# High and low activation halves in one 512-column product, in both FFNs and layer 1's output projection

## The chip, the core and the metric

The kernel runs on one core of a Trainium2 chip. The metric is the device time of one execution in microseconds. Five engines run their own instruction streams in order and meet through semaphores: TensorE (PE; its weight loads have a row of their own, PEld), VectorE (DVE), ScalarE (ACT), GpSimd (POOL) and SyncE (SP, which here issues nearly all transfers).

## The reference

Two decoder layers over 256 tokens of width 2048, in float32. Layer 0 mixes tokens with RWKV-7 and Gated DeltaNet, layer 1 with Mamba-2; each mixer has an input and an output projection, and each layer ends in a SwiGLU feed-forward block (FFN) of hidden width 5632. Every sub-layer is normalised, scaled and shifted by vectors made from `c` and a weight matrix ("ada"), and added back through a gate. What the change touches is the FFN of both layers and the last line of the Mamba-2 mixer:

```python
def swiglu(h, w1, w3, w2):
    return (jax.nn.silu(h @ w1) * (h @ w3)) @ w2
...
    return y.astype(h.dtype) @ w_out          # mamba2_mix: 4096 -> 2048
...
        x = x + gate * y
        shift, scale, gate = ada_modulation(c, ada_ffn_w[i], ada_ffn_b[i])
        h = rms_norm(x) * (1.0 + scale) + shift
        x = x + gate * swiglu(h, ffn_w1[i], ffn_w3[i], ffn_w2[i])
```

## The kernel before

Activations lie with features on the 128 partitions and the 256 tokens (T) along the free side, so a matrix of width 2048 is 16 tiles of 128x256. Every large product is made in float32r, whose operands are rounded; to keep float32 accuracy each operand is split into a high and a low part, and a 128x128 weight tile is used in three matmuls of 256 columns: high weights by high activations, high weights by low activations, low weights by high activations. In the program `whi` and `wlo` are the parts of the weights, `hhi`/`hlo`, `ghi`/`glo`, `yhi`/`ylo` those of the activations (normed input, FFN hidden layer, second half of the mixer's output).

Weights stream from memory. `pieces` lists them in order of use; `issue_raw` has SP load each into one of five `raw` buffers; `split_next` has ScalarE copy a piece of up to 8 weight tiles (128x1024) into `whi`; `low_parts` has VectorE write `raw - whi` into `wlo`. There are three buffers each of `whi` and `wlo` (`PARTS`), so ScalarE's copy of a piece waits until TensorE has left the piece three before it. `products` writes the matmuls of a piece: for unit i (one weight tile) the two with `whi`, and LAG = 4 units later the one with `wlo`.

An FFN runs in two halves of 22 hidden tiles. The *up* stage makes, for each hidden tile, the gate and the value product (16 units each) in the two halves of one 512-column bank; ScalarE applies Silu to the gate (`fs`), VectorE multiplies (`fg`), and `split` makes `ghi` and `glo`. The first 8 of the 88 up products of each FFN run apart, in `lin_slab`, which goes through all eight per input tile while the input is still being normed; the change leaves them alone. The *down* stage makes 16 output tiles of 22 units each in the first half of a bank; `out_tiles` adds each to the residual `x` through the gate. Layer 1's output projection has 16 output tiles in each of two halves of 16 units.

Beside this, VectorE makes the ada vectors: 320 half rows `adat` of 128x1024, multiplied and summed by one custom instruction each, spread over layer 0, its FFN, the Mamba-2 mixer, layer 1's output projection and the start of layer 1's FFN.

The order of the instructions on each engine is fixed when the program is written: a `Clock` class with costs per instruction form decides how far ahead pieces are split (`SOON`), when an ada half row is put into VectorE's stream (`fill_ada`, which lets it in when VectorE is early by that clock, or when it is due) and when the mixers' step chains take a step (`run`). The costs count columns: a 512-column float32r matmul costs 217.6 ns in it, two of 256 columns 217.6 together. What the change adds to VectorE and ScalarE therefore also moves the ada rows and the steps of layer 1's mixer; layer 0's mixer stands as it was.

Of the kernel before, what the change touches and what calls it, by code (L numbers as in the profile page):

```python
# [395 lines left out]
def trunk(ctx: ExitStack, tc: tile.TileContext, I, out):  # L396
# [117 lines left out]
    hhi = cp.tile([P, KT, T], F32R, name="hhi")  # L514
    hlo = cp.tile([P, KT, T], F32R, name="hlo")
    h2 = (hhi, hlo)
# [232 lines left out]
    def products(units, hi, lo, o, act):  # L749

        ahi, alo = act
        n = len(units)
        lag = min(LAG, n)
        w = lambda t, i: t[:, (o + i) * P:(o + i + 1) * P]
        for i in range(n + lag):
            if i < n:
                ps, kt, a, z = units[i]
                PE.matmul(ps, w(hi, i), ahi[:, kt, :], start=a, stop=False)
                PE.matmul(ps, w(hi, i), alo[:, kt, :], start=False, stop=False)
            if i >= lag:  # L760
                ps, kt, a, z = units[i - lag]
                PE.matmul(ps, w(lo, i - lag), ahi[:, kt, :], start=False, stop=z)
            if i % STEP == STEP - 1 or i == n + lag - 1:
                low_parts()
                issue_raw()
                run()
                if max(clock.at(ET.DVE), clock.at(ET.Activation)) < clock.at(ET.PE) + SOON:
                    prefetch()
                fill_ada()
# [86 lines left out]
    def out_tiles(l, m, ps, x, nxt=None):  # L856

        ms = range(m, m + len(ps))
        for o, m in zip(ps, ms):
            V.scalar_tensor_tensor(x[:, m, :], o, modc(l, 2, m), x[:, m, :], ALU.mult, ALU.add)  # L860
# [16 lines left out]
    def ffn(l, x, told, tnew):  # L877
# [4 lines left out]
        with tc.tile_pool(name=f"ffn{l}", bufs=1, reuse_waits="tile") as fp:  # L882
            ghi = fp.tile([P, NHH, T], F32R, name=f"ghi{l}")
            glo = fp.tile([P, NHH, T], F32R, name=f"glo{l}")
            for half in range(2):
                for jj in range(NHH):
                    if pss:
                        ps = pss.pop(0)
                    else:
                        ps = bank(True)  # L890
                        for q in range(2):
                            lin_tile(ps[:, q * T:(q + 1) * T], h2, range(KT))
                    s = fp.tile([P, T], F32, tag="fs", name=nm("fs"), bufs=2)
                    g = fp.tile([P, T], F32, tag="fg", name=nm("fg"), bufs=2)
                    S.activation(s, ps[:, 0:T], AF.Silu)
                    V.tensor_tensor(g, s, ps[:, T:2 * T], ALU.mult)
                    release(ps)
                    split(ghi[:, jj, :], glo[:, jj, :], g)
                for m in range(16):
                    ps = bank(True)  # L900
                    for q in range(2):
                        lin_tile(ps[:, 0:T], (ghi, glo), range(11 * q, 11 * q + 11), q == 0, q == 1)
                    out_tiles(l, m, [ps[:, 0:T]], x, (l + 1, t) if half == 1 else None)
                    release(ps)
# [775 lines left out]
    def layer1(x, told):  # L1680
# [4 lines left out]
        with tc.tile_pool(name="y1", bufs=1, reuse_waits="tile") as yp:  # L1685
            ymix = yp.tile([P, 32, T], F32, name="ymix1")
            with tc.tile_pool(name="mx1", bufs=1, reuse_waits="tile") as mx:
# [3 lines left out]
                for m in range(16):  # L1691
                    ps = bank(True)
                    lin_tile(ps[:, 0:T], h2, range(KT))
                    out_tiles(2, m, [ps[:, 0:T]], x)
                    release(ps)
                drain()
            t = open_x("t1")
            with tc.tile_pool(name="yo1", bufs=1, reuse_waits="tile") as fp:
                yhi = fp.tile([P, KT, T], F32R, name="yhi1")
                ylo = fp.tile([P, KT, T], F32R, name="ylo1")  # L1700
                for kt in range(KT):
                    split(yhi[:, kt, :], ylo[:, kt, :], ymix[:, 16 + kt, :])
                for m in range(16):
                    ps = bank(True)
                    lin_tile(ps[:, 0:T], (yhi, ylo), range(KT))
                    out_tiles(2, m, [ps[:, 0:T]], x, (3, t))
# [273 lines left out]
```

## Time and profile before

| | us |
|---|---|
| median of 3 runs (lowest, highest) | 3013.86 (3011.43, 3022.01) |
| the profiled execution: its own time | 3014.75 |
| its span | 3012.9 |
| mean granted TensorE clock | 0.981 of full speed |

| stage (us from the start) | PE busy | DVE busy | ACT busy |
|---|---|---|---|
| FFN 0, up, first half (840 to 1040) | 200.00 | 149.36 | 86.66 |
| FFN 0, down, first half (1040 to 1160) | 120.00 | 100.34 | 49.05 |
| FFN 0, up, second half (1160 to 1410) | 250.00 | 176.25 | 108.26 |
| Mamba-2 mixer (1560 to 2100) | 533.63 | 447.14 | 319.73 |
| layer 1's output projection (2120 to 2240) | 119.21 | 91.98 | 59.13 |
| FFN 1, up, second half (2630 to 2870) | 240.00 | 120.60 | 105.04 |
| FFN 1, down, second half (2870 to 2995) | 125.00 | 68.28 | 61.08 |

Since matmuls overlap in the records (one of 281 ns starts every 117 ns or so), "busy" only says that TensorE had no hole there; how fast it went is read from the number of matmuls in a stretch. Nearly all instructions are recorded under one line, L372 of the helper that keeps the order, so groups are told apart by the tiles that they write and read.

### The profile page before, as it was taken

Reading aid. Unit: us, or ns where it says so; the run is one execution under the profiler, and the core shown is the slowest. Engines: PE = TensorE matmul, PEld = TensorE weight load, DVE = VectorE, ACT = ScalarE, POOL = GpSimd, SP = SyncE. Lnnn points to the kernel's source line nnn. Section 1 sums busy time; section 2 is a strip of 40 time slices with the busy share of each in tenths; the row PEclk is TensorE's granted clock in tenths of the full one; section 3 lists DMA queues with packets and bytes.
Section 4 is the critical chain, followed back from the end, with each engine's and each line's share of the span. In section 5 each row is a group of like instructions: output and inputs, shape, how many; then the busy total and the mean of one; then the engine's idle time right before and its main releaser. Section 6 shows DMA issues by size and latency. Waiting matters only on the chain.

```text
span 3012.9 us, 61369 instructions
## 1 busy us (share of the span) xinstructions
PE 2884.7 (96%) x25095; PEld 2816.0 (93%) x25095; DVE 2199.6 (73%) x3438; ACT 1440.2 (48%) x2358; POOL 172.5 (6%) x191
## 2 busy tenths in 40 slices
PE   6789999998799999999999999999999999999998
PEld 6788889888699999999999999999999999999998
DVE  6987888888677787677768878888867745554555
ACT  3354546544344444444456556555445444444444
POOL 3400101100000000000000111111000000000000
PEclk9998999999899999999999999999999999999999
DMA  9865565577687898877865666666866755655554
GB/s 396 345 199 176 173 221 162 174 251 260 223 320 278 286 332 308 285 270 261 261 221 200 207 213 229 214 233 218 281 225 236 273 185 174 200 184 191 185 174 153
DMA packets 236730, 706.29 MB, mean 234 GB/s; under 512 B 36848, under 2 KB 55584, under 8 KB 236192
## 3 DMA queue, kind: packets, MB, share of 16 engines
q1 hardware_dynamic: 235872, 699.46, 67.9%
q8 instruction: 196, 3.21, 0.4%
q10 hardware_dynamic: 576, 2.92, 0.2%
q14 instruction: 86, 0.70, 0.1%
HBM read 695.70 MB, written 6.58 MB: 233 GB/s over the span
## 4 chain that ended last, share of the span: by engine, by line
issue 52%; PE 21%; DVE 2%; ACT 1%; DMA 0%; POOL 0%; DVEq 0%; POOLq 0%; ACTq 0%
PE bank L372 21%; DVE wlo L372 1%; ACT whi L372 0%; DMA adat<-in_ada 0%; DVE w L372 0%; DVE ymix L372 0%; DVE x L372 0%; POOL mgsa L372 0%; ACT mar L372 0%; DVE adat L372 0%; DVE mar L372 0%; ACT t L372 0%; DVE mxs L372 0%; DVE hlo L372 0%; DVE t0b L372 0%
## 5 line engine op out<-in xcount | busy, mean ns | idle before, releaser
L372 PE MATMUL bank<-hhi,whi 128*128 128x256 f32 x5568 | 1477.5, 287 | 35.3 <-ACT whi L372 33.9
L372 PE MATMUL bank<-hlo,whi 128*128 128x256 f32 x5568 | 1455.1, 283 | 6.9 <-DVE hlo L372 6.9
L372 DVE TENSOR_TENSOR wlo<-raw,whi 128x1024 fp32r<-128x1024 f32 (+3 forms) x1001 | 1112.5, 1125 | 438.8 <-ACT whi L372 433.6
L372 ACT ACTIVATE whi<-raw 128x1024 fp32r<-128x1024 f32 (+3 forms) x1001 | 967.9, 975 | 683.5 <-PE bank L372 659.5
L372 PE MATMUL bank<-hhi,wlo 128*128 128x256 f32 x5568 | 1126.6, 284 | 31.1 <-DVE wlo L372 30.9
L372 PEld LDWEIGHTS bank<-hhi,whi 128*128 128x128 f32 x5568 | 1064.0, 191 | 53.9 <-ACT whi L372 39.6
L372 PEld LDWEIGHTS bank<-hlo,whi 128*128 128x128 f32 x5568 | 1063.9, 191 | 10.4 <-DVE hlo L372 8.5
L372 PEld LDWEIGHTS bank<-hhi,wlo 128*128 128x128 f32 x5568 | 861.8, 190 | 41.7 <-DVE wlo L372 36.1
L372 PE MATMUL bank<-glo,whi 128*128 128x256 f32 x1408 | 351.1, 281 | 0.0
L372 PE MATMUL bank<-ghi,whi 128*128 128x256 f32 x1408 | 351.0, 281 | 0.0
L372 PEld LDWEIGHTS bank<-glo,whi 128*128 128x128 f32 x1408 | 265.0, 188 | 0.0
L372 PEld LDWEIGHTS bank<-ghi,whi 128*128 128x128 f32 x1408 | 265.0, 188 | 0.0
L372 PE MATMUL bank<-ghi,wlo 128*128 128x256 f32 x1408 | 229.6, 281 | 0.0
L372 DVE CUSTOM_DVE_ANT_0 adat<-adat,silc,adap 128x1024 f32<-128x1024 f32 x160 | 211.7, 1323 | 20.2 <-DMA adat<-in_ada 19.2
L372 DVE CUSTOM_DVE_ANT_0 adat<-adat,silc,prm 128x1024 f32<-128x1024 f32 x160 | 208.5, 1303 | 11.9 <-DMA adat<-in_ada 11.5
L372 PEld LDWEIGHTS bank<-ghi,wlo 128*128 128x128 f32 x1408 | 193.8, 188 | 0.0
L372 ACT ACTIVATE fs<-bank 128x256 f32<-128x256 f32 x88 | 33.9, 385 | 194.7 <-PE bank L372 194.7
L372 DVE TENSOR_TENSOR fg<-fs,bank 128x256 f32<-128x256 f32 x88 | 37.0, 420 | 111.5 <-ACT fs L372 111.5
L372 DVE SCALAR_TENSOR_TENSOR w<-pad,prm,w 128x256 f32<-128x256 f32 x216 | 110.0, 510 | 5.2
L372 POOL TENSOR_TENSOR rstd<-rpow,half_neg 128x2 f32<-128x2 f32 x5 | 3.5, 696 | 1774.2 <-DVE rpow L372 1774.2
L372 DVE CUSTOM_DVE_ANT_0 ini<-ini,silc,prm 128x2048 f32<-128x2048 f32 x32 | 84.7, 2646 | 15.9 <-DMA prm<-in_prm 15.9
L372 DVE SCALAR_TENSOR_TENSOR x<-bank,mod,x 128x256 f32<-128x256 f32 x106 | 50.6, 481 | 48.1 <-PE bank L372 48.0
(253 smaller groups left out, 2043.4 us busy)
## 6 DMA issues: line engine op xcount, KB each, us to landing
raw<-in_ffn SPq DMA_DIRECT2D x352, 512.0 KB, 4.6
adat<-in_ada SPq DMA_DIRECT2D x320, 512.0 KB, 4.8
raw<-in_in SPq DMA_DIRECT2D x238, 512.0 KB, 3.5
raw<-in_ffn SPq DMA_DIRECT2D x128, 384.0 KB, 3.6
raw<-in_ffn SPq DMA_DIRECT2D x128, 320.0 KB, 4.5
raw<-in_out SPq DMA_DIRECT2D x75, 512.0 KB, 4.9
ini<-in_ada SPq DMA_DIRECT2D x32, 1024.0 KB, 8.2
raw<-in_in SPq DMA_DIRECT2D x48, 448.0 KB, 5.2
```

The costliest lines, as they stand in the source:

```text
L372: r = f(*a, **k)
```

## The change

The two parts of an activation tile are put side by side: `hc`, `gc` and `yc` are tiles of 16 or 22 times 512 columns, with the high part in columns 0 to 255 and the low part in 256 to 511. Where the bank handed to `products` is 512 columns wide, one matmul of 512 columns through the high weight tile takes the place of the two of 256; the matmul with the low weights goes to the bank's first half. So the first half of the bank ends with high by high plus low by high, the second half with high weights by low activations, and the two halves are added afterwards: in the up stage by a ScalarE copy of the second half (`fu`) and a VectorE add of the first half to it, for the gate (into `fs`, then Silu in place) and for the value (into `fg`, then the product); in `out_tiles` by adding both halves to `x`, one after the other. An up product now has a bank of its own.

```diff
-    hhi = cp.tile([P, KT, T], F32R, name="hhi")
-    hlo = cp.tile([P, KT, T], F32R, name="hlo")
-    h2 = (hhi, hlo)
+    def hi_lo(pool, name, n):
+
+        q = pool.tile([P, n, 2 * T], F32R, name=name)
+        return q[:, :, 0:T], q[:, :, T:2 * T], q
+
+    h2 = hi_lo(cp, "hc", KT)
+    hhi, hlo = h2[:2]
...
     def products(units, hi, lo, o, act):
...
-                PE.matmul(ps, w(hi, i), ahi[:, kt, :], start=a, stop=False)
-                PE.matmul(ps, w(hi, i), alo[:, kt, :], start=False, stop=False)
+                if ps.shape[-1] == 2 * T:
+
+                    PE.matmul(ps, w(hi, i), both[:, kt, :], start=a, stop=False)
+                else:
+                    PE.matmul(ps, w(hi, i), ahi[:, kt, :], start=a, stop=False)
+                    PE.matmul(ps, w(hi, i), alo[:, kt, :], start=False, stop=False)
             if i >= lag:
                 ps, kt, a, z = units[i - lag]
-                PE.matmul(ps, w(lo, i - lag), ahi[:, kt, :], start=False, stop=z)
+                PE.matmul(ps[:, 0:T], w(lo, i - lag), ahi[:, kt, :], start=False, stop=z)
...
     def out_tiles(l, m, ps, x, nxt=None):
-            V.scalar_tensor_tensor(x[:, m, :], o, modc(l, 2, m), x[:, m, :], ALU.mult, ALU.add)
+            for i in range(0, o.shape[-1], T):
+                V.scalar_tensor_tensor(x[:, m, :], o[:, i:i + T], modc(l, 2, m), x[:, m, :], ALU.mult, ALU.add)
...
     def ffn(l, x, told, tnew):
-                        ps = bank(True)
-                        for q in range(2):
-                            lin_tile(ps[:, q * T:(q + 1) * T], h2, range(KT))
-                    S.activation(s, ps[:, 0:T], AF.Silu)
-                    V.tensor_tensor(g, s, ps[:, T:2 * T], ALU.mult)
-                    release(ps)
+                        u = fp.tile([P, T], F32, tag="fu", name=nm("fu"), bufs=2)
+                        for o in (s, g):
+                            ps = bank(True)
+                            lin_tile(ps, h2, range(KT))
+                            S.activation(u, ps[:, T:2 * T], AF.Copy)
+                            V.tensor_tensor(o, ps[:, 0:T], u, ALU.add)
+                            release(ps)
+                            if o is s:
+                                S.activation(s, s, AF.Silu)
+                                u = fp.tile([P, T], F32, tag="fu", name=nm("fu"), bufs=2)
+                        V.tensor_tensor(g, s, g, ALU.mult)
                     split(ghi[:, jj, :], glo[:, jj, :], g)
...
-                        lin_tile(ps[:, 0:T], (ghi, glo), range(11 * q, 11 * q + 11), q == 0, q == 1)
-                    out_tiles(l, m, [ps[:, 0:T]], x, (l + 1, t) if half == 1 else None)
+                        lin_tile(ps, g2, range(11 * q, 11 * q + 11), q == 0, q == 1)
+                    out_tiles(l, m, [ps], x, (l + 1, t) if half == 1 else None)
```

How the order of the instructions moves is shown at three places. First TensorE, in an up product of FFN 0 (`bank` is the accumulator, `whi` and `wlo` the weights); before, the last units of a piece of 8:

```order
L372 MATMUL bank_76<-hhi,wlo_14795 128x256
L372 MATMUL bank_76<-hhi,whi_14794 128x256
L372 MATMUL bank_76<-hlo,whi_14794 128x256
L372 MATMUL bank_76<-hhi,wlo_14795 128x256
L372 MATMUL bank_76<-hhi,whi_14794 128x256
L372 MATMUL bank_76<-hlo,whi_14794 128x256
L372 MATMUL bank_76<-hhi,wlo_14795 128x256 x5
```

and a whole piece of the change:

```order
L372 MATMUL bank_75<-hc,whi_12069 128x512 x5
L372 MATMUL bank_75<-hc,wlo_12070 128x256
L372 MATMUL bank_75<-hc,whi_12069 128x512
L372 MATMUL bank_75<-hc,wlo_12070 128x256
L372 MATMUL bank_75<-hc,whi_12069 128x512
L372 MATMUL bank_75<-hc,wlo_12070 128x256
L372 MATMUL bank_75<-hc,whi_12069 128x512
L372 MATMUL bank_75<-hc,wlo_12070 128x256 x5
```

Each pair through a high tile has become one matmul; the lag of four units stays.

Second, ScalarE in the up stage of FFN 0, before, from one hidden tile to the next:

```order
L372 ACTIVATE fs_14143<-bank_72 128x256
L372 ACTIVATE ghi_8672<-fg_14144 128x256
L372 ACTIVATE whi_14160<-raw_100 128x1024
L372 ACTIVATE whi_14179<-raw_101 128x1024
L372 ACTIVATE whi_14209<-raw_102 128x1024
L372 ACTIVATE whi_14242<-raw_103 128x1024
L372 ACTIVATE fs_14270<-bank_73 128x256
```

and now:

```order
L372 ACTIVATE whi_13175<-raw_102 128x1024
L372 ACTIVATE whi_13190<-raw_98 128x1024
L372 ACTIVATE fu_13165<-bank_69 128x256
L372 ACTIVATE fs_13163<-fs_13163 128x256
L372 ACTIVATE whi_13216<-raw_99 128x1024
L372 ACTIVATE whi_13234<-raw_100 128x1024
L372 ACTIVATE fu_13211<-bank_74 128x256
L372 ACTIVATE gc_8671<-fg_13164 128x256
```

There is a bank to read after every two weight pieces instead of after every four, and both times a second instruction follows that waits for VectorE before the next piece is split.

Third, VectorE in the first down stage of FFN 0, before, from one output tile to the next (the `ISA` rows on `adat` are ada half rows, those that write only `mod` or `adap` read the sum out):

```order
L372 SCALAR_TENSOR_TENSOR x_7676<-bank_74,mod,x_7676 128x256
L372 TENSOR_TENSOR wlo_11199<-raw_102,whi_11198 128x768
L372 TENSOR_TENSOR wlo_11223<-raw_103,whi_11222 128x640
L372 ISA adat_114,mod<-adat_114,silc,adap_11192 128x1024
L372 ISA mod 128x1
L372 TENSOR_SCALAR mod<-mod 128x1
L372 TENSOR_TENSOR wlo_11245<-raw_99,whi_11244 128x768
L372 TENSOR_TENSOR wlo_11269<-raw_100,whi_11268 128x640
L372 ISA adat_113,adap_11279<-adat_113,silc,prm 128x1024
L372 ISA adap_11279 128x1
```

and now:

```order
L372 SCALAR_TENSOR_TENSOR x_7675<-bank_70,mod,x_7675 128x256 x2
L372 TENSOR_TENSOR wlo_10882<-raw_98,whi_10881 128x768
L372 TENSOR_TENSOR wlo_10899<-raw_99,whi_10898 128x640
L372 ISA adat_112,adap_10909<-adat_112,silc,prm 128x1024
L372 ISA adap_10909 128x1
L372 TENSOR_TENSOR wlo_10916<-raw_100,whi_10915 128x768
L372 ISA adat_113,mod<-adat_113,silc,adap_10909 128x1024
L372 ISA mod 128x1
L372 TENSOR_SCALAR mod<-mod 128x1
L372 TENSOR_TENSOR wlo_10936<-raw_101,whi_10935 128x640
```

A tile has two residual adds, four low parts and two ada half rows where it had one, four and two. Over the whole program the ada rows drift: ahead of layer 1's first weight load stood 237 of the 320 ada loads in SP's order, and now 225; ahead of its output projection's first 272, and now 271.

More of the change, by code (lines that the diff above doesn't have):

```diff
@@ L749, in products @@
     def products(units, hi, lo, o, act):
-        ahi, alo = act
+        ahi, alo, both = act
         n = len(units)
@@ L882, in ffn @@
         with tc.tile_pool(name=f"ffn{l}", bufs=1, reuse_waits="tile") as fp:
-            ghi = fp.tile([P, NHH, T], F32R, name=f"ghi{l}")
-            glo = fp.tile([P, NHH, T], F32R, name=f"glo{l}")
+            g2 = hi_lo(fp, f"gc{l}", NHH)
+            ghi, glo = g2[:2]
             for half in range(2):
                 for jj in range(NHH):
+                    s = fp.tile([P, T], F32, tag="fs", name=nm("fs"), bufs=2)
+                    g = fp.tile([P, T], F32, tag="fg", name=nm("fg"), bufs=2)
                     if pss:
                         ps = pss.pop(0)
-                    else:
-                        ps = bank(True)
-                        for q in range(2):
-                            lin_tile(ps[:, q * T:(q + 1) * T], h2, range(KT))
-                    s = fp.tile([P, T], F32, tag="fs", name=nm("fs"), bufs=2)
-                    g = fp.tile([P, T], F32, tag="fg", name=nm("fg"), bufs=2)
-                    S.activation(s, ps[:, 0:T], AF.Silu)
-                    V.tensor_tensor(g, s, ps[:, T:2 * T], ALU.mult)
-                    release(ps)
+                        S.activation(s, ps[:, 0:T], AF.Silu)
+                        V.tensor_tensor(g, s, ps[:, T:2 * T], ALU.mult)
+                        release(ps)
+                    else:
+                        u = fp.tile([P, T], F32, tag="fu", name=nm("fu"), bufs=2)
[4 more added lines that the diff above has]
+                            V.tensor_tensor(o, ps[:, 0:T], u, ALU.add)
+                            release(ps)
+                            if o is s:
+                                S.activation(s, s, AF.Silu)
+                                u = fp.tile([P, T], F32, tag="fu", name=nm("fu"), bufs=2)
+                        V.tensor_tensor(g, s, g, ALU.mult)
                     split(ghi[:, jj, :], glo[:, jj, :], g)
@@ L1692, in layer1 @@
                     ps = bank(True)
-                    lin_tile(ps[:, 0:T], h2, range(KT))
-                    out_tiles(2, m, [ps[:, 0:T]], x)
+                    lin_tile(ps, h2, range(KT))
+                    out_tiles(2, m, [ps], x)
                     release(ps)
@@ L1698, in layer1 @@
             with tc.tile_pool(name="yo1", bufs=1, reuse_waits="tile") as fp:
-                yhi = fp.tile([P, KT, T], F32R, name="yhi1")
-                ylo = fp.tile([P, KT, T], F32R, name="ylo1")
+                y2 = hi_lo(fp, "yc1", KT)
+                yhi, ylo = y2[:2]
                 for kt in range(KT):
@@ L1704, in layer1 @@
                     ps = bank(True)
-                    lin_tile(ps[:, 0:T], (yhi, ylo), range(KT))
-                    out_tiles(2, m, [ps[:, 0:T]], x, (3, t))
+                    lin_tile(ps, y2, range(KT))
+                    out_tiles(2, m, [ps], x, (3, t))
                     release(ps)
```

## The prediction

> **What bounds the kernel now.** I read the page's table of slices first, then the windows by stage, then the timeline inside one stage. TensorE decides: its row of tenths is 9 nearly everywhere from the second quarter on, and in the stages that the change touches it has no hole. In the view of windows the columns are the stretch, its length, then busy time and (x) records of PE, PEld, DVE, ACT, POOL, the granted clock, the DMA share and GB/s:
>
> ```profile
> PE   6789999998799999999999999999999999999998
> 1060.00:1160.00 100.00, 100.00 (x845) 100.00 (x844) 82.47 (x123) 41.08 (x50) 0.00 (x0) 1.00 0.95 339
> 2320.00:2500.00 180.00, 180.00 (x1537) 180.00 (x1536) 109.54 (x129) 78.65 (x96) 0.00 (x0) 1.00 0.68 230
> 2520.00:2620.00 100.00, 100.00 (x845) 100.00 (x844) 50.65 (x65) 40.61 (x51) 0.00 (x0) 1.00 0.61 189
> 2660.00:2860.00 200.00, 200.00 (x1707) 200.00 (x1706) 100.71 (x107) 87.98 (x107) 0.00 (x0) 1.00 0.58 187
> ```
>
> The clock is 1.00 here, so the throttle is no part of it. The counts give the beat: a record lasts 281 ns, so about 2.4 of those counted began before the stretch. In up stages 180 / (1537 - 2.4) = 117.3 ns a matmul, in down stages 100 / (845 - 2.4) = 118.7. VectorE and ScalarE are at 50% and 44% in FFN 1, and VectorE at 82% in FFN 0's first down stage, where it also makes ada rows.
>
> What is a beat made of? The timeline in an up stage, matmuls and weight loads:
>
> ```profile
> 2700.04 0.28 PE L372 MATMUL bank<-hhi,whi 128*128 128x256 f32 x1
> 2700.04 0.19 PEld L372 LDWEIGHTS bank<-hlo,whi 128*128 128x128 f32 x1
> 2700.15 0.28 PE L372 MATMUL bank<-hlo,whi 128*128 128x256 f32 x1
> 2700.16 0.19 PEld L372 LDWEIGHTS bank<-hhi,whi 128*128 128x128 f32 x1
> 2700.27 0.28 PE L372 MATMUL bank<-hhi,whi 128*128 128x256 f32 x1
> ```
>
> Every matmul has its own weight load, also the second one through the same high tile, and the load of the next begins with the start of the one before. Matmul and load thus take turns in a chain of 0.11 to 0.12 us, and either could be the longer. Two rows tell which:
>
> ```profile
> 176.12 0.74 PEld L372 LDWEIGHTS bank<-la,lora 128*128 128x128 f32 x4
> 176.24 1.03 PE L372 MATMUL bank<-la,lora 128*128 128x256 f32 x4
> L372 PE MATMUL bank<-la,lora x32: 378/379/796, 176.2 to 520.3; 128*128 128x256 f32 x32
> 617.78 0.38 PE L372 MATMUL bank<-zeros 128*128 128x512 f32 x1
> 618.00 0.28 PE L372 MATMUL bank<-hhi,whi 128*128 128x256 f32 x1
> 638.11 0.38 PE L372 MATMUL bank<-zeros 128*128 128x512 f32 x1
> 638.33 0.28 PE L372 MATMUL bank<-hhi,whi 128*128 128x256 f32 x1
> ```
>
> A float32 product of 256 columns, each record two passes over them, starts every (1.03 - 0.38) / 3 = 0.217 us; the float32r matmul of 512 columns that clears a bank is followed 0.22 us later, at the full clock, twice. So 512 columns behind one load cost about 217 ns, and two matmuls of 256 cost 2 x 117.3 = 234.7 or 2 x 118.7 = 237.3. What the bare stream costs shows where the throttle granted half the clock, in the stall at FFN 0's start:
>
> ```profile
> 827.20:829.30 2.10, 2.10 (x11) 2.10 (x11) 2.10 (x3) 0.65 (x1) 0.00 (x0) 0.50 0.52 154
> 827.20 0.41 PE L372 MATMUL bank<-hlo,whi 128*128 128x256 f32 x1
> ...
> 829.33 0.41 PE L372 MATMUL bank<-hhi,whi 128*128 128x256 f32 x1
> ```
>
> Ten matmuls in 2.13 us, 213 ns each, so 106.7 at the full clock: the beat of 117.3 or 118.7 has 10.6 or 12 ns on top of the stream, which vanish where the stream is slow. My reading: at 256 columns a weight load is a little longer than the stream and sets the beat; at 512 it is hidden.
>
> **The change, part by part.** *TensorE.* In `products` a unit was three matmuls and becomes one of 512 columns and one of 256. The one of 256 still has the next tile's load beside it, so I leave it at 117.3 or 118.7. Up: 3 x 117.3 = 352.0 before, 217 + 117.3 = 334.3 after, 17.7 ns less. Down: 356.0 and 335.7, 20.4 ns less. How many units:
>
> ```profile
> L372 PE MATMUL bank<-ghi,whi 128*128 128x256 f32 x1408 | 351.0, 281 | 0.0
> L372 PE MATMUL bank<-yhi,whi 128*128 128x256 f32 x256 | 66.6, 281 | 0.0
> 2140.00:2240.00 100.00, 99.21 (x833) 98.86 (x832) 75.54 (x108) 51.62 (x79) 0.00 (x0) 1.00 0.75 252
> ```
>
> 1408 units go down in the two FFNs. Layer 1's output projection has 256 with `yhi` and as many in its first half with `hhi`, and goes at the down beat (833 records in 99.21 us of work). Up products are 88 less the 8 of the slab, of 16 units, in two FFNs: 2560. So 2560 x 17.7 = 45.3 us and (1408 + 512) x 20.4 = 39.2 us, together **84.5 us** less.
>
> The 512-column matmul of this change moves real data, where the clearing one reads a single column 512 times; that is the price the trace doesn't show. Its bounds: at worst what lies above the stream belongs to the columns and 512 cost 235 to 237 (saving 0); at best the 256-column matmul loses its excess too, down to the 109 ns at which a load and a short matmul follow each other here (0.60 less 0.27 for the last, over 3):
>
> ```profile
> 1730.08 0.60 PE L372 MATMUL bank<-cst,mxs 128*128 128x128 f32 x4
> ```
>
> Then a unit is 217 + 109 = 326, 26 and 30 ns less, 2560 x 26 + 1920 x 30 = 124 us. I take 217 and 117 to 119, since the clearing rows are float32r with the same neighbours.
>
> By the Trainium skill, "TensorE: Matmul & The Clock Gate", section "Back-to-back issue gap", an isolated warm matmul costs its columns at 2.4 GHz and 2.5 ns, that is 109 ns at 256 and 216 at 512, so that joining two would save 2.5 ns, some 11 us over these 4480 units (an estimate from that page). The 512-column row agrees with it; the beat of 117.3 and 118.7 doesn't, and the measurement decides.
>
> *ScalarE and VectorE.* Added are a ScalarE copy and a VectorE add for each of 160 up products, and a second residual add for each of 64 down and 32 projection tiles:
>
> ```profile
> L372 ACT ACTIVATE fs<-bank 128x256 f32<-128x256 f32 x88 | 33.9, 385 | 194.7 <-PE bank L372 194.7
> L372 DVE TENSOR_TENSOR fg<-fs,bank 128x256 f32<-128x256 f32 x88 | 37.0, 420 | 111.5 <-ACT fs L372 111.5
> L372 DVE SCALAR_TENSOR_TENSOR x<-bank,mod,x 128x256 f32<-128x256 f32 x106 | 50.6, 481 | 48.1 <-PE bank L372 48.0
> L372 ACT ACTIVATE whi<-raw 128x1024 fp32r<-128x1024 f32 x71 | 75.2, 1059 | 61.1 <-PE bank L372 60.2 <-ACT whi L372 0.3
> ```
>
> That is 160 x 0.385 = 62 us on ScalarE, and 160 x 0.42 + 96 x 0.48 = 113 us on VectorE, all beside matmuls. In FFN 1 it is covered: ScalarE's idle time there ends on TensorE (60.2 of 61.1 us ahead of `whi`), not the other way round. What waits behind the new ScalarE instructions is the next piece's split. Before, in FFN 0:
>
> ```profile
> 1187.28 0.39 ACT L372 ACTIVATE fs<-bank 128x256 f32<-128x256 f32 x1 [2.38 <-PE bank L372]
> 1188.15 0.42 ACT L372 ACTIVATE ghi<-fg 128x256 fp32r<-128x256 f32 x1 [0.49 <-DVE fg L372]
> 1188.47 2.17 ACT L372 ACTIVATE whi<-raw 128x1024 fp32r<-128x1024 f32 x2
> 1189.55 2.36 DVE L372 TENSOR_TENSOR wlo<-raw,whi 128x1024 fp32r<-128x1024 f32 x2 [0.53 <-ACT whi L372]
> ```
>
> The piece split first at 1188.47 is done by 1189.53, its low part by 1190.8. TensorE then holds two split pieces of 8 x 0.334 = 2.67 us, so it needs this one 5.3 us after the tile's end near 1187.2, at 1192.5, and the low part four units later. The new add puts 0.42 us and a hand-over into this chain; over 2 us of slack are left, and one ada half row (1.28 us) in a bad place still fits.
>
> The thin place is FFN 0's down stage, with two ada half rows a tile:
>
> ```profile
> L372 DVE CUSTOM_DVE_ANT_0 adat<-adat,silc,adap 128x1024 f32<-128x1024 f32 x14 | 17.9, 1280 | 2.5 <-DMA adat<-in_ada 2.5
> L372 DVE SCALAR_TENSOR_TENSOR x<-bank,mod,x 128x256 f32<-128x256 f32 x12 | 5.8, 480 | 4.0 <-PE bank L372 4.0
> ```
>
> VectorE's 82.47 us in 100 are 6.46 in a tile of 22 x 0.356 = 7.83; with another 0.48 it is 6.94 in 7.39, 94%. Bounds: nothing, or one uncovered half row in each of the 32 tiles, 41 us; I take 5, as two pieces wait ready. Transfers there run at 339 GB/s; the same bytes in 6% less time are 360, and in the start-up, the core moved 396 in the first of these slices:
>
> ```profile
> GB/s 396 345 199 176 173 221 162 174 251 260 223 320 278 286 332 308 285 270 261 261 221 200 207 213 229 214 233 218 281 225 236 273 185 174 200 184 191 185 174 153
> ```
>
> Layer 1 gets some 11 half rows more by the new order, 14 us of VectorE, and a reshuffled mixer: bounds -10 and 14, I take 4. At three stage ends the last tile's second add is bare, 1.5 us. Together 10.5 us more.
>
> The sum: 3014.75 - 84.5 + 10.5 = 2940.75; the profiled execution stands 0.9 above the median of the runs, so I say 2940.
>
> **The rivals.** *A fixed cost per matmul.* The 10.6 or 12 ns above the stream belong to every matmul whatever its length. Then a 512 costs 224 or 225 and only one excess goes: 2560 x 10.6 + 1920 x 12 = 50 us, 3014.75 - 50 + 10.5 = 2975. For it speaks that the two stages differ in a constant; against it the 0.22 and 0.217. 12%. *Both excesses go:* 3014.75 - 124 + 10.5 = 2901. For it, that two loads instead of three press on the same memory; against it, that the lone 256 keeps its neighbouring load. 6%. *The excess goes with the columns:* 512 real columns cost 235, nothing is saved, 3014.75 + 10.5 = 3025; the clearing rows speak against it. 6%. *VectorE becomes the bound in FFN 0:* two ada half rows ahead of a low part and of the new add, in the 80 tiles of its up and the 32 of its down stage. It decides where VectorE brings a low part later than two pieces (5.3 us) after the tile's end; at 0.9 us for each of 112 tiles it eats 100 us, and 3014.75 - 84.5 + 100 = 3030. VectorE's 94% speaks for it, its slack in up stages against it. 5%. That the matmuls aren't joined is excluded: the new order has the 512-column rows.
>
> **How the numbers follow.** 71% for the forecast (its own range 2920 to 2960). Of a measurement here 0.5%, 15 us, can be told from no change. Faster is 71 + 12 + 6 = 89%, same the 6% of the column rival, slower the 5% of VectorE. The range of 8 in 10 takes in the first rival above and the second below: 2900 to 2985.
>
> **What would show it.** In the profile after: 128x512 groups with 4480 records, a stretch of FFN 1's up stage with about 2 / 334.3 ns = 5.98 records a microsecond in place of 8.52, and a down stage with 5.96 in place of 8.43. In the timeline the 256 follows its 512 after 0.217 us and the next 512 follows that after 0.117. PE without holes in FFN 1; in FFN 0 holes behind `wlo` of at most some microseconds. A start-to-start of 0.235 would prove the column rival, PE waits on `wlo` of tens of microseconds the VectorE one.

## The result: slower, by less than one per cent

| | before | after |
|---|---|---|
| median of the runs on one chip (lowest, highest) | 3012.64 us (3009.92, 3022.01) | 3036.88 us (3033.42, 3039.80) |
| the profiled execution: its own time | 3014.75 us | 3039.80 us |
| its span | 3012.9 us | 3038.0 us |

The ratio is 1.0081, with a 95% interval of 1.0064 to 1.0098. Forecast were 2940 us, and 2900 to 2985 as the range: the direction is wrong, and the time lies 52 us above the range's end.

First the windows of the changed kernel in FFN 1: the first up stage, the first down stage and the second up stage (columns as in the prediction: stretch, length, then busy time and records of PE, PEld, DVE, ACT, POOL, granted clock, DMA share, GB/s).

```profile
2400.00:2500.00 100.00, 100.00 (x574) 87.30 (x573) 72.80 (x98) 48.97 (x73) 0.00 (x0) 1.00 0.75 256
2540.00:2640.00 100.00, 100.00 (x571) 87.11 (x570) 57.26 (x78) 41.24 (x52) 0.00 (x0) 1.00 0.66 188
2670.00:2870.00 200.00, 200.00 (x1149) 174.79 (x1147) 114.70 (x144) 98.12 (x144) 0.00 (x0) 1.00 0.59 189
```

There is no hole, and the clock is 1.00, as before. A unit is now two records. Of those counted about 1.9 began before the stretch, so an up unit takes 200 / ((1149 - 1.9) / 2) = 348.7 ns and a down unit 100 / ((571 - 1.9) / 2) = 351.4 ns. Before they took 352.0 and 356.0; forecast were 334.3 and 335.7. The timeline in that up stage shows which of the two matmuls is the longer one:

```profile
2702.51 1.33 PE L372 MATMUL bank<-hc,whi 128*128 128x512 f32 x5
2703.68 0.28 PE L372 MATMUL bank<-hc,wlo 128*128 128x256 f32 x1
2703.80 0.39 PE L372 MATMUL bank<-hc,whi 128*128 128x512 f32 x1
2704.03 0.28 PE L372 MATMUL bank<-hc,wlo 128*128 128x256 f32 x1
2704.14 0.39 PE L372 MATMUL bank<-hc,whi 128*128 128x512 f32 x1
```

Five of 512 columns in a row start (1.33 - 0.39) / 4 = 0.235 us apart; the lone 256 is followed after 0.11 to 0.12 us, as before. A start-to-start of 0.235 is what the prediction named as proof of its column rival.

That explains a missing gain and not yet a loss. The loss stands in one place. From the start of each matmul in the trace, the stages are, in us:

| stage | before | after |
|---|---|---|
| up to FFN 0 (same program) | 745.9 | 747.2 |
| FFN 0: up, down, up, down | 281.7, 125.3, 250.6, 130.4 | 285.3, 123.7, 245.8, 131.6 |
| layer 1 from its first weights to its projection's second half | 620.5 | 648.0 |
| that second half | 96.8 | 96.7 |
| FFN 1: up, down, up, down | 250.3, 125.3, 247.8, 129.1 | 253.0, 123.7, 245.8, 128.0 |

Layer 1 takes 27.5 us more, all the rest together about 2 us less (one profile of each kernel). The Mamba-2 mixer, which the change doesn't edit, pays. TensorE's waits in this stretch (engine, line and tile, what it waited for: us in total, times, longest), before:

```profile
PE bank L372 <- POOL mgsa L372: 2.5, 1, 2.5
PE bank L372 <- DVE wlo L372: 1.6, 3, 0.8
PE bank L372 <- DVE mar L372: 1.4, 1, 1.4
```

and after:

```profile
PE bank L372 <- ACT whi L372: 13.1, 9, 3.2
PE bank L372 <- DVE mar L372: 8.4, 2, 5.8
PE bank L372 <- DVE wlo L372: 3.2, 4, 1.6
```

The three rows shown are 5.5 us before and 24.7 us after; with the smaller rows it is 5.9 and 28.9. `mar` is a step of the mixer's chain, `whi` the next split weights. Most of it happens early: windows of the mixer's start, before,

```profile
1634.00:1734.00 100.00, 97.97 (x856) 94.96 (x855) 86.04 (x130) 62.23 (x115) 16.73 (x13) 1.00 0.60 202
1734.00:1934.00 200.00, 199.06 (x1714) 193.53 (x1713) 165.49 (x247) 118.67 (x219) 27.06 (x19) 1.00 0.66 226
```

and after:

```profile
1634.00:1734.00 100.00, 84.32 (x710) 79.67 (x709) 76.34 (x119) 55.60 (x109) 15.54 (x12) 0.97 0.51 171
1734.00:1934.00 200.00, 198.27 (x1709) 192.77 (x1708) 169.46 (x255) 116.20 (x208) 23.07 (x18) 1.00 0.66 226
```

In the first of these windows TensorE does 146 matmuls fewer, in the next 200 us only 5. At 117.3 ns each, that is 18 us, and by the counts of the 100 us ahead (824 before, 799 after) another 3; the rest of the 27.5 us is lost behind 1934 us, where TensorE waits for `whi` once more (5.1 us in all). VectorE isn't busier in the first window but less busy: it waits too, since the mixer's steps hand on from engine to engine. What has come into its stream are ada half rows; VectorE's groups in the mixer's first 166 us, before,

```profile
L372 DVE CUSTOM_DVE_ANT_0 adat<-adat,silc,adap 128x1024 f32<-128x1024 f32 x2 | 5.6, 2820 | 0.0
L372 DVE CUSTOM_DVE_ANT_0 adat<-adat,silc,prm 128x1024 f32<-128x1024 f32 x3 | 3.8, 1277 | 0.0
```

and after:

```profile
L372 DVE CUSTOM_DVE_ANT_0 adat<-adat,silc,adap 128x1024 f32<-128x1024 f32 x7 | 9.0, 1279 | 0.1
L372 DVE CUSTOM_DVE_ANT_0 adat<-adat,silc,prm 128x1024 f32<-128x1024 f32 x7 | 8.9, 1276 | 1.2 <-DMA adat<-in_ada 1.2
```

14 half rows where there were 5. The additional ones came early: ahead of 1634 us there are 9 where there was 1, and in the window of the 146 missing matmuls 7 where there were 6.

### The profile page after: what moved, and what is told of

It is laid out like the page before. It is cut to its first block, busy times and chain, and to the rows that moved or that the text cites. A ratio compares the mean times of both kernels' runs of the same rounds, so it can differ in the third digit from the quotient of the medians.

```text
span 3038.0 us, 52784 instructions
## 1 busy us (share of the span) xinstructions
PE 2876.6 (95%) x20615; PEld 2599.5 (86%) x20615; DVE 2299.3 (76%) x3694; ACT 1477.8 (49%) x2518; POOL 170.0 (6%) x191
## 5 line engine op out<-in xcount | busy, mean ns | idle before, releaser
L372 PE MATMUL bank<-hc,whi 128*128 128x256 f32 (+1 forms) x8320 | 1724.2, 325 | 63.4 <-ACT whi L372 53.9
L372 PEld LDWEIGHTS bank<-hc,whi 128*128 128x128 f32 x8320 | 1273.3, 192 | 181.4 <-ACT whi L372 63.7
L372 PE MATMUL bank<-hc,wlo 128*128 128x256 f32 x5568 | 1125.7, 284 | 34.4 <-DVE wlo L372 34.2
L372 PEld LDWEIGHTS bank<-hc,wlo 128*128 128x128 f32 x5568 | 886.4, 190 | 79.0 <-DVE wlo L372 43.1
L372 PE MATMUL bank<-gc,whi 128*128 128x512 f32 x1408 | 384.8, 395 | 0.0
L372 PEld LDWEIGHTS bank<-gc,whi 128*128 128x128 f32 x1408 | 246.7, 188 | 41.5
L372 PEld LDWEIGHTS bank<-gc,wlo 128*128 128x128 f32 x1408 | 211.2, 188 | 23.0 <-DVE wlo L372 0.7
L372 PE MATMUL bank<-gc,wlo 128*128 128x256 f32 x1408 | 229.0, 281 | 0.3 <-DVE wlo L372 0.3
L372 ACT ACTIVATE fu<-bank 128x256 f32<-128x256 f32 x160 | 61.5, 384 | 327.4 <-PE bank L372 327.4
L372 PE MATMUL bank<-yc,whi 128*128 128x512 f32 x256 | 77.9, 401 | 1.5 <-DVE yc L372 1.5
```

The source lines that it names most:

```text
L372: r = f(*a, **k)
```

## The experiments

Rival causes had to be told apart each time. On TensorE: the excess over the bare stream comes from the weight load (the prediction), from the accumulation in the bank, or from fetching the moving columns. On layer 1: the ada rows that FFN 0 no longer takes cost the mixer its time, or something else in the change does (new buffers, banks, more records). "Stages" are those of the table above. Where a ratio with an interval stands, several runs were timed against the kernel before; else it is a single run.

**What sets the beat.** `e1_beat512` is the changed kernel with another operand in each of FFN 1's four stages: a moving operand of one column read over and over, a weight tile of one zero column, no accumulation, and different columns that are all zero. `e2_beat256` has the same in the kernel before.

```diff
+        def w(t, i):
+            return zeros.to_broadcast([P, P]) if md == "zero_w" else t[:, (o + i) * P:(o + i + 1) * P]
+        def mov(kt, n):
+            if md == "col":
+                return both[:, kt, 0:1].to_broadcast([P, n])
+            return zrow[0][:, 0:n] if md == "zero_x" else both[:, kt, 0:n]
+        fr = md == "fresh"
...
-                    PE.matmul(ps, w(hi, i), both[:, kt, :], start=a, stop=False)
+                    PE.matmul(ps, w(hi, i), mov(kt, 2 * T), start=a or fr, stop=fr)
```

> The changed kernel with four things tried in the four stages of layer 1's FFN; its output is not the reference's. In the first up stage every matmul reads one moving column over and over (a step of 0) in place of 512 or 256 different ones; in the first down stage the weight tile is one zero column read 128 times; in the second up stage every matmul overwrites its bank and none accumulates; in the second down stage the moving operand is a tile of 512 different columns that all hold zero. In the changed kernel a 512 is followed by the next matmul after 229 to 234 ns in all four. If the excess over 213 comes from fetching different moving columns: 215 to 220 in the first up stage alone, 229 to 234 in the other three. If it comes from the weight load that runs beside: 215 to 220 in the first down stage alone. If from adding into the bank: in the second up stage alone. If from the values (power): in the second down stage, and 229 in the first up stage, whose column holds real values. The lone matmul of 256 stays at 117 to 119 in the first up stage if the weight load sets it, as the prediction had it, and falls to 107 to 110 if fetching does.

> The same four variants in layer 1's FFN of the kernel before (all matmuls 256 columns; the output is not the reference's), which goes there at 117.3 ns a matmul in the up and 118.7 in the down stages. If the weight load sets the beat, as the prediction had it: first up stage (one moving column) 117, first down stage (one weight column) 107 to 110. If fetching moving columns does: first up stage 107 to 110, first down stage 118.7. Adding into the bank: the second up stage falls to 107 to 110. Values: the second down stage falls.

Windows of `e1_beat512` in the four stages, in the order named:

```profile
2400.00:2500.00 100.00, 100.00 (x614) 91.91 (x613) 76.32 (x104) 51.19 (x76) 0.00 (x0) 1.00 0.79 273
2530.00:2630.00 100.00, 100.00 (x577) 87.50 (x577) 54.67 (x79) 41.08 (x52) 0.00 (x0) 1.00 0.57 189
2660.00:2860.00 200.00, 200.00 (x1147) 174.73 (x1146) 114.53 (x144) 99.26 (x144) 0.00 (x0) 1.00 0.58 189
2900.00:3000.00 100.00, 100.00 (x571) 87.12 (x570) 62.12 (x91) 48.69 (x78) 0.00 (x0) 1.00 0.59 189
```

and of `e2_beat256`:

```profile
2400.00:2480.00 80.00, 80.00 (x719) 80.00 (x718) 45.02 (x50) 37.05 (x46) 0.00 (x0) 1.00 0.64 203
2510.00:2610.00 100.00, 100.00 (x835) 100.00 (x835) 47.55 (x65) 39.79 (x51) 0.00 (x0) 1.00 0.54 179
2640.00:2840.00 200.00, 200.00 (x1707) 200.00 (x1706) 100.59 (x107) 87.86 (x108) 0.00 (x0) 1.00 0.59 187
2890.00:2990.00 100.00, 100.00 (x845) 100.00 (x844) 55.33 (x77) 49.09 (x77) 0.00 (x0) 1.00 0.58 178
```

Read as before, these counts are, per unit of 512 and 256, 326.7, 347.8, 349.3 and 351.4 ns, and per matmul of 256 columns 111.6, 120.1, 117.3 and 118.7 ns. Only the first variant of each got clearly faster. Its timeline in `e1_beat512`:

```profile
2451.54 0.27 PE L372 MATMUL bank<-hc,wlo 128*128 128x256 f32 x1
2451.65 0.38 PE L372 MATMUL bank<-hc,whi 128*128 128x512 f32 x1
2451.87 0.27 PE L372 MATMUL bank<-hc,wlo 128*128 128x256 f32 x1
```

With one column read over and over the joined matmul is followed after 217 ns, the lone one after 110, and the three of before after 112 each, although their weight loads are as they were. Weights of one column, no accumulation and zeros in all columns leave the beat within 1.5% of what it was. So neither the weight load nor the bank nor the values set the beat; reading different columns of the moving operand does. The reading "a weight load is a little longer than the stream and sets the beat" falls, and with it the price of 217 ns: it came from clearing matmuls, which read a single column.

**What it is about the columns.** `e11_columns` tells a cost per column from a cost per address: in FFN 1's first up stage 256 columns, each read twice in a row; in the first down stage 64 columns, gone through eight times; in the second up stage every second column, 256 of them twice over, so that a matmul walks over double the addresses; in the second down stage nothing.

```diff
+            if md == "twice":
+                return both[:, kt, 0:n // 2].unsqueeze(2).to_broadcast([P, n // 2, 2])
+            if md == "cycle":
+                return both[:, kt, 0:64].unsqueeze(1).to_broadcast([P, n // 64, 64])
+            if md == "step2":
+                return both[:, kt, 0:512:2] if n == T else both[:, kt, 0:512:2].unsqueeze(1).to_broadcast([P, 2, T])
```

> The changed kernel with other moving columns in layer 1's FFN (output not the reference's): in the first up stage 256 columns each read twice in a row, in the first down stage the same 64 columns read over and over, in the second up stage every second column (a step of 8 bytes). One column read 512 times took 216 ns, 512 different ones in a row 229 to 234. If a repeat of the column just read is what saves: the first up stage lies between, 222 to 226, the first down stage stays at 229 to 234. If few different columns suffice: the first down stage falls to 216. If the bytes apart matter: the second up stage is slower than 234.

Windows of its first three stages:

```profile
2400.00:2500.00 100.00, 100.00 (x613) 91.87 (x612) 76.05 (x102) 52.17 (x78) 0.00 (x0) 1.00 0.81 274
2530.00:2630.00 100.00, 100.00 (x571) 87.14 (x570) 57.24 (x79) 41.24 (x52) 0.00 (x0) 1.00 0.66 189
2700.00:2900.00 200.00, 200.00 (x586) 121.86 (x585) 59.83 (x73) 50.97 (x74) 0.00 (x0) 1.00 0.28 95
```

and the timeline of the third:

```profile
2800.22 2.45 PE L372 MATMUL bank<-hc,whi 128*128 128x512 f32 x5
2802.72 0.63 PE L372 MATMUL bank<-hc,whi 128*128 128x512 f32 x1
2803.17 0.42 PE L372 MATMUL bank<-hc,wlo 128*128 128x256 f32 x1
```

A column read twice in a row costs as little as one read 512 times (a unit of 327.3 ns; 222 to 226 ns for its 512 columns were expected, they took 217); 64 columns gone through again and again gain nothing (351.4 ns), so nothing is kept of what was read a while ago; and every second column takes (2.45 - 0.63) / 4 = 455 ns for 512 where neighbours take 229 to 235. The stage took 482.2 us instead of 245.8, with the clock at 1.00. In bytes of address per partition that is 2048 / 232 = 8.8 a nanosecond in the plain walk and 4096 / 455 = 9.0 with every second column left out. These two walks, and the repeats that cost nothing, fit one account: the moving operand is fetched at about 9 bytes of address a nanosecond and partition, and where the bare stream of 0.424 ns a column (217 / 512) asks for more (4 / 0.424 = 9.4), the fetch sets the beat. Steps above two were not tried, so whether it goes on by bytes or by larger pieces of memory stays open.

This also accounts for a row that had misled: at half the granted clock the prediction read 213 ns for 256 columns, no excess. There the stream asks for 1024 / 213 = 4.8 bytes a nanosecond, which the fetch gives. So the fetch isn't halved with the clock: that would be 4.4 bytes, and 2 x 117.3 = 235 ns a matmul. How much more than 4.8 it could give there isn't shown.

By the Trainium skill, "SBUF — State Buffer", section "A bandwidth-pool intuition that's wrong (but worth ruling out)", the moving operand has its own read path of some 614 GB/s, stated for two-byte elements, and weight loads a second, independent one. The independence agrees with the one-column weights (347.8 against 351.4 ns a unit); the figure doesn't carry over to four-byte operands, which came here at 128 x 2048 bytes / 232 ns = 1130 GB/s.

**What joining is worth.** `e7_two256` is the change in all but the joined matmul: the same tiles, banks and extra adds, with two matmuls of 256 into the two halves of the bank.

```diff
-                    PE.matmul(ps, w(hi, i), both[:, kt, :], start=a, stop=False)
+                    PE.matmul(ps[:, 0:T], w(hi, i), ahi[:, kt, :], start=a, stop=False)
+                    PE.matmul(ps[:, T:2 * T], w(hi, i), alo[:, kt, :], start=False, stop=False)
```

> All of the change except the joining: each high weight tile is used in two matmuls of 256 columns, one into each half of the bank; tiles, adds and the order of the ada rows stay (222 ahead of layer 1, 46 in the mixer). It measures what the joined matmul itself brings. By the beats read in the changed kernel (a unit of 349 us/1000 up and 351 down, where three matmuls took 352 and 356) it should be slower than the change by 2560 x 3 ns + 1920 x 5 ns, 17 us, 3045 to 3058. If joining brought the 85 us of the prediction and something else ate them: 3100 or more. If it brings nothing: 3037.

It ran in 3053.95 us, so joining brings 3053.95 - 3036.88 = 17 us (a single run against a median). The beats say the same: (352.0 - 348.7) x 2560 + (356.0 - 351.4) x 1920 = 17.3 us. The joined matmul does gain, a fifth of the 84.5 us forecast. Without it layer 1 takes 648.5 us, so its 27.5 us don't come from the joined matmul.

**Where layer 1's time went.** `e3_ffn0_before` has FFN 0 as before and the rest changed.

```diff
-                    if pss:
-                        ps = pss.pop(0)
+                    if l == 1 or pss:
+                        if pss:
+                            ps = pss.pop(0)
+                        else:
+                            ps = bank(True)
+                            for q in range(2):
+                                lin_tile(ps[:, q * T:(q + 1) * T], h2, range(KT))
...
+                    pt = ps[:, 0:T] if l == 1 else ps
```

> Layer 0's FFN as in the kernel before, everything else as changed, so that 234 of the 320 ada rows stand ahead of layer 1 as before, and not 222. The change lost 28 us between the start of layer 1 and its projection's second half (620 to 648 us). Theory: the rows that slipped out of layer 0's FFN into the mixer are due there, are let in although VectorE is late, and hold up the mixer's chain. Then this kernel has 620 us there and all of it takes about 3010 us, 3 less than before. Rival: the tile with both parts side by side, or the wider projection, slows the mixer itself: 3035.

It ran in 3008.32 us (5 us less than before; ratio 0.9988, 0.9974 to 1.0002, so it can't be told from the kernel before), with 621.4 us in layer 1, and as many ada rows ahead of layer 1 as the kernel before. The loss comes from FFN 0's form. The planner lets an undue ada row into VectorE's stream only where VectorE stands 500 ns ahead by its clock. With the extra adds it hardly ever does, FFN 0 takes the due rows alone, and 12 rows more are left for layer 1. To show that this suffices, `e5_before_due` makes that one thing happen in the kernel before, with nothing of the change in it:

```diff
+    fill_at = [FILL]
...
-                until = clock.at(ET.PE) + (LATE if due <= st["item"] else FILL)
+                until = clock.at(ET.PE) + (LATE if due <= st["item"] else fill_at[0])
...
+        fill_at[0] = -1e9 if l == 1 else FILL
```

> The kernel before, with no 512-column matmul, in which layer 0's FFN takes only ada rows that are due and none ahead of time: 222 rows stand ahead of layer 1, as in the changed kernel, and not 234, and 46 between its input and its output projection, as in the change, not 35. Theory (the slipped rows hold up the mixer's start): layer 1 up to the second half of its projection takes 640 to 650 us in place of 620, and the kernel 3033 to 3042, though nothing of the change is in it. Rival (the change itself slows the mixer, its tiles or its order): 620 and 3013.

It ran in 3038.32 us, 1.0081 of the kernel before (1.0065 to 1.0097), with 646.9 us in layer 1 and these waits of TensorE there:

```profile
PE bank L372 <- ACT whi L372: 13.5, 9, 3.2
PE bank L372 <- DVE mar L372: 8.4, 2, 5.8
PE bank L372 <- DVE wlo L372: 3.0, 3, 1.5
```

That is 26.4 of layer 1's 27.5 us, with nearly the same waits, and no matmul is changed. (That its total comes so near to the change's 3036.88 is chance: what the change gains by joining it loses again in other stages.) The reverse is `e6_fill500`: the whole change, with FFN 0 letting undue rows in as long as VectorE is no more than 500 ns late (`fill_at[0] = 500 if l == 1 else FILL` in the same place).

> The whole change, and in layer 0's FFN alone an ada row is let in up to 500 ns before VectorE is early (it must be 500 ns early otherwise), which brings the rows back to 234 ahead of layer 1 and 35 in the mixer. Theory: the mixer's stretch falls from 648 to 620 or 622 us and the kernel to 3005 to 3012; layer 0's FFN takes at most 3 us more. Rival: the order with the change's VectorE work cannot hold these rows, layer 0's FFN is held up by 15 us or more, and the time stays above 3025.

It ran in 3002.05 us, 0.9961 of before (0.9948 to 0.9975), with 619.9 us in layer 1, and there:

```profile
PE bank L372 <- POOL mgsa L372: 2.5, 1, 2.5
PE bank L372 <- DVE wlo L372: 1.6, 4, 0.8
PE bank L372 <- DVE mar L372: 1.4, 1, 1.4
```

So with the rows back in FFN 0 the change is a gain of 12 us by the medians. By the stages it is less: from FFN 0 on its profile is 5.0 us shorter than that of the kernel before, and another 3.9 us lie ahead of FFN 0, where the programs are the same; that part varied between 740.6 and 749.7 us over the profiles of all these kernels.

What the runs don't separate is the rows from the order that the planner makes around them. With the rows it also arranges the mixer's steps otherwise: by the tiles that they write and read, at most 540 of ScalarE's 616 instructions of the kernel before in this stretch stand in the same sequence in `e5_before_due`, and as many in the change. In `e6_fill500` and `e3_ffn0_before` all 616 do. During TensorE's longest wait in the change, 5.8 us for `mar` up to 1671 us, VectorE has no ada row (none from 1650 to 1689 us); the steps ahead of `mar` had come late. No run keeps the steps' order and moves the rows alone.

**Moving the rows the other way** didn't help. `e4_due_later` leaves FFN 0 alone and makes layer 1's rows due 46 weight pieces later, so that the mixer isn't made to take them.

```diff
-        adaq.extend(r + (len(seq) + int(DUE * i * len(w) / len(a)),) for i, r in enumerate(a))
+        adaq.extend(r + (len(seq) + late + int(DUE * i * len(w) / len(a)),) for i, r in enumerate(a))
```

> The whole change, but the ada rows of layer 1 are due 46 pieces of weights later, so that 34 of them (35 before, 46 in the change) stand between layer 1's first weight load and that of its projection. Theory (the slipped rows hold up the mixer): its stretch goes from 648 back to 620 to 625 us, and all of it takes 3007 to 3015. Rival (any new order of the mixer's steps is worse than the tuned one, whatever the rows): the stretch stays near 640 to 650 and the time near 3035.

Layer 1 came back to 620.7 us, as expected, but the time was 3038.89 us (1.0085, 1.0064 to 1.0106), not 3007 to 3015: the rows came up at FFN 1's start, whose first up stage took 279.3 us instead of 253.0. The planner's order of the mixer's steps differs from the kernel before here too (574 of ScalarE's 616 in sequence), and layer 1 lost nothing by it, so a new order alone need not cost. At FFN 1's start TensorE waits 20.6 us for weight pieces (2.2 in the change), and ScalarE, which splits these, for the vectors `mod` that the late rows make:

```profile
PE bank L372 <- ACT whi L372: 20.6, 9, 5.8
...
ACT hc L372 <- DVE mod L372: 29.7, 5, 7.5
```

The rows are a fixed load; a stretch that takes fewer leaves them to the next.

**Better versions.** `e8_down500` takes the joined matmul in the down stages and the projection alone, where it costs one add in place of a copy and an add, with the rule of `e6_fill500`.

> The wide matmul only in the down stages and layer 1's output projection (1920 units), the up stages with three matmuls of 256 and no copy and add, and the ada rows of layer 0's FFN let in as in the run with 500 ns, so that 234 stand ahead of layer 1. If the wide units bring 4 to 5 ns each and the mixer keeps its 620 us: 1920 x 4.5 ns = 9 us less than before, 3000 to 3007, the fastest of all. If the up stages' wide units are worth more than their extra VectorE work: slower than the whole change with 500 ns.

It ran in 3014.72 us (0.9999, 0.9988 to 1.0010), a miss: the up stages do pay. Against `e6_fill500` each second up stage took 247.8 us instead of 245.8 and FFN 1's first 256.7 instead of 253.0, while FFN 0's first took 283.3 instead of 285.6. From FFN 0 on that makes 5.1 of the 10.1 us between the two profiles; the other 5.0 lie ahead of FFN 0. `e9_fill_out` is `e6_fill500` with undue rows let in 500 ns late in layer 1's projection too (`fill_at[0] = 500.0` at its start), which leaves fewer for FFN 1.

> The whole change with the rows let in 500 ns late in layer 0's FFN (as in the run that took 3002 us) and in layer 1's output projection too, so that 295 rows stand ahead of layer 1's FFN as in the kernel before, and not 288. Theory (rows due in a stage's start cost it time): layer 1's FFN loses the 2.7 us by which its first up stage was longer than before (253.0 against 250.3), 2999 to 3001. If those 2.7 us are the wide up stage's own (ScalarE waiting behind VectorE): 3002 as without it.

FFN 1's first up stage went from 253.0 to 249.7 us as meant; the time, 3002.77 us (0.9960, 0.9945 to 0.9974), can't be told from that of `e6_fill500` (its profile had 6.1 us more ahead of FFN 0 and 4.0 less from there on). What was left in FFN 0's up stage shows in the timelines of VectorE and ScalarE in `e6_fill500`:

```profile
838.76 1.28 DVE L372 CUSTOM_DVE_ANT_0 adat<-adat,silc,adap 128x1024 f32<-128x1024 f32 x1
839.97 0.42 DVE L372 TENSOR_TENSOR fs<-bank,fu 128x256 f32<-128x256 f32 x1
...
836.19 0.42 ACT L372 ACTIVATE gc<-fg 128x256 fp32r<-128x256 f32 x1 [3.56 <-DVE fg L372]
840.42 0.42 ACT L372 ACTIVATE fs<-fs 128x256 f32<-128x256 f32 x1 [2.21 <-DVE fs L372]
840.75 1.04 ACT L372 ACTIVATE whi<-raw 128x1024 fp32r<-128x1024 f32 x1
```

The Silu waits 2.21 us for VectorE's add, which sits behind an ada row, and the next weight split waits behind the Silu. `e10_silu_later` is `e9_fill_out` with the Silu put behind the value product's copy, where its operand has long been there:

```diff
-                            if o is s:
+                            if o is g:
                                 S.activation(s, s, AF.Silu)
+                            else:
                                 u = fp.tile([P, T], F32, tag="fu", name=nm("fu"), bufs=2)
```

> As the one above, and Silu of the gate stands one product later in ScalarE's stream, behind the copy of the value product's second half, so that it never waits for VectorE's add. In the change ScalarE waited 48 us for that add, and in layer 0's FFN TensorE waited some 6 us for split weights in the first half's up stage. If that wait is what holds the split back: the first up stage of layer 0's FFN falls from 285.6 to 281 to 283 us and the whole to 2996 to 2999. If the wait for the value's product (88 us) does: no change.

It ran in 2995.93 us (2993.33 to 2998.00), 0.9940 of the kernel before (0.9926 to 0.9953), the fastest of all. FFN 0's first up stage took 283.8 us (before 281.7, with the change 285.3, in `e6_fill500` 285.6), a little over the 281 to 283 that were expected; layer 1 took 617.5 and FFN 1's first up stage 248.8. Against the kernel before the medians differ by 18 us; of the 19.9 us between the profiles 14.5 lie from FFN 0 on, and 5.3 ahead of it.

## Why the prediction was wrong

**The bound** was read rightly: TensorE without holes at the full clock, also in the changed kernel.

**The price of 512 columns** failed: "So 512 columns behind one load cost about 217 ns", taken "since the clearing rows are float32r with the same neighbours". Measured are 229 to 235. The text itself said that the clearing matmul reads one column 512 times; that very property made it fast. The other row, the float32 product with 0.217, reads different columns, but passes over them twice in a record; if it passes twice over a column before the next, it is the case "each read twice" above. That would fit; it was not tried. The term was sized 84.5 us and is 17; its lower bound of 0 held it, the choice between the bounds was wrong. Of the 99 us between the sum of 2940.75 and the profiled 3039.80 this is 67.

**The lone 256** stayed at 117 to 118 ns, as taken. **The half-clock row** was measured rightly and read wrongly: it shows that the excess doesn't scale with the stream, which a fetch of fixed pace does as well as a weight load. The variant with one-column weights would have been the test; no row of the trace before could make it.

**Layer 1's rows and its reshuffled mixer** failed too: "bounds -10 and 14, I take 4". The rows were counted (237 ahead of layer 1 before, 225 after) and priced at VectorE's own time, 11 half rows, 14 us. The cost was 27.5 us, twice the upper bound, and 24 more of the 99. `e5_before_due` gives 646.9 - 620.5 = 26.4 with the rows moved and nothing else of the change. In the mixer's start, VectorE's work stands in a chain of steps from engine to engine; with 9 more rows there (14 for 5), and the order of steps that the planner makes with them, the steps and the weight splits behind them come late, up to 5.8 us in one wait. The upper bound took the row's own time for all that a row can cost, and the reshuffling for harmless; how the 26.4 us divide between the two stays open.

**The FFNs' extras** were about right in size and wrong in place. Forecast were 5 us in FFN 0's down stages; the first took 123.7 us, 352 x 351.4 ns, with nothing lost, and the second lost 2.8. FFN 0's first up stage took 285.3 us for 281.7, where its 576 units should have brought 1.9 us, so 5.5 us were lost there. TensorE's waits for `whi` in it grew by 2.1 us only (21.5 to 23.6), so the cause is shown in part: late adds, as the VectorE rival had it, and not its 100. FFN 1, which the text held covered, lost 4.6 in its first up stage, which `e9_fill_out` wins back 3.3 of (249.7) by moving ada rows.

**The rivals.** The column rival had the mechanism (6%) and a time of 3025, with 11 us for the extras; with 17 us gained and layer 1's 27.5 lost it is 3014.75 - 17 + 27.5 = 3025 again, by coincidence. The 14.5 us that remain to the profiled 3039.8 are, by the stages against what their units should bring, 5.5 and 4.6 in the first up stages of the two FFNs, 2.8 in FFN 0's last down stage and 1.3 by which the unchanged part ran longer; the differences of the other stages nearly cancel. The unchanged part varied by 9 us over the kernels, so a few us of this sum are open. The fixed cost per matmul, 2975, fell with the beat of 235, "both excesses go", 2901, with 349 ns a unit; its 326 ns came only where a column is read again at once (326.7 and 327.3). The chance of slower, 5%, was placed on VectorE in FFN 0 alone. A rival "the rows go to the mixer and cost more than their own time" was in the text only as a term with bounds and should have been one with a chance.

**The Trainium skill's rule** cited ("TensorE: Matmul & The Clock Gate", "Back-to-back issue gap") put the gain of joining at 2.5 ns a matmul, some 11 us, against 17 measured; its 216 ns for 512 columns hold here only where each column is read at least twice in a row (217), and 512 different ones take 229 to 235.

## What to carry to other kernels

A price for a matmul must come from a row that reads the same kind of operand: a repeated column, or a clearing matmul, streams faster than different four-byte columns (217 ns against 229 to 235 for 512), and joining two matmuls over one weight tile saved only 3 to 5 ns here, where the moving operand's fetch sets the beat. Where a planner fills an engine's idle time with a fixed load, ask of any added work where that load goes, and price it where it lands and not at its own length: here 12 rows more for layer 1, with the order that the planner made of its steps, cost 26 us. A change that is slower as it stands may be worth keeping once the planner's threshold is moved with it: 3036.88 became 2995.93 us by three edits to the order of the work.

## What was not expected of the hardware

A float32r moving operand came here at about 9 bytes of address a nanosecond and partition: 512 neighbouring columns take 229 to 235 ns, every second column 455, a column read twice in a row 217 for 512. A step of 2 in the moving operand thus cost double, with the clock at 1.00 and no wait in the trace.

The beat of plain stages differs a little without a known cause: FFN 0's second up stage took, with the same matmuls, 250.6 us in the profile before (118.7 ns a matmul) and 247.8 in that of `e3_ffn0_before` (117.3), so that 2.8 of the 4.8 us that this stage gains by the change need not come from joining; and zero values take the same 118.7 ns as real ones in a down stage. Which of the tiles' addresses or the bank makes 117.3 or 118.7 of it stays open.
